# A trunk kernel on one Trainium2 core: two stage boundaries run one tile of 128 tokens at a time, in a fixed order

## The chip, the cores and the metric

The kernel runs on one core of one Trainium2 chip. The metric is the device time of one execution in microseconds (us). A core has TensorE for matrix products (PE in the profile; its weight loads are PEld), VectorE (DVE), ScalarE (ACT), GpSimd (POOL) and SyncE (SP), which here issues all the DMAs. Each engine works through its own queue in order, and waits on semaphores for the others. Results of PE land in PSUM, which has 8 banks of 128x512 f32; everything else on the chip lies in SBUF.

## The reference

Two decoder layers over 256 tokens of width 2048, batch 1, in f32. Layer 0 mixes by causal pooling, layer 1 by multi-head latent attention with 16 heads; both end in a SwiGLU FFN of width 5632. Between the layers one latent (512 wide) and one rotary key are computed from the stream and shared by all heads.

```
for i in range(DEPTH):
    shift_m, scale_m, gate_m, shift_f, scale_f, gate_f = split(silu(c) @ mod_w[i] + mod_b[i], 6)
    if i == 1:
        kv_shift, kv_scale = split(silu(c) @ kv_mod_w + kv_mod_b, 2)
        h_kv = rmsnorm(x, kv_in_norm) * (1 + kv_scale) + kv_shift
        ckv = rmsnorm(h_kv @ w_dkv, kv_norm)           # then ckv @ w_uk, ckv @ w_uv; h_kv @ w_kr is roped
    h = rmsnorm(x, norm_mix[i]) * (1 + scale_m) + shift_m
    y = pool_mixer(h) if i == 0 else mla_mixer(h, kv)  # mla_mixer ends in  o @ w_o
    x = x + gate_m * y
    h = rmsnorm(x, norm_ffn[i]) * (1 + scale_f) + shift_f
    x = x + gate_f * ((silu(h @ w_gate) * (h @ w_up)) @ w_down)
return rmsnorm(x, final_norm)
```

So at two places the whole stream x must be finished before its norm is known, and the norm before the next products can begin: from the FFN of layer 0 to the latent (`h_kv @ w_dkv`), and from attention (`o @ w_o`) to the FFN of layer 1.

## The kernel before

**Tiles.** The 256 tokens are two tiles of 128 (NT = 2), the width is four blocks of 512 (ND = 4, CH = 512). A weight block is 512x512 f32, 1 MB. It is loaded into a `raw` buffer (6 of them), and `split` makes two parts of it: `hi`, rounded by ACT to the fast format float32r (L427), and `lo`, the remainder, by DVE (L429); both go to `hl` buffers (6, three pairs). Activations are held in the same two parts. `proj_unit` (L446) multiplies one block with both token tiles: hi·hi, hi·lo, lo·hi, four products of 128x128 by 128x512 each, 12 for each tile, 24 for the block (L451). In the last block of a sum the 12 of tile 0 stand ahead of the 12 of tile 1.

**The background.** The modulation vectors need 12 products of the vector c with 2048-wide weights. They run as background units: each unit loads 1 MB into a `raw` buffer and adds it on DVE (L238, 128x2048, or L311 in two instructions of 128x1024). `split` calls `tick`, which issues units at a planned rate beside the weight blocks (`plan`, `release`, `pump`); `hold` stops it. Ahead of the latent, nine units are kept back (`MLA_LATE`) and released over the next weight blocks (`MLA_UNITS` = 6).

**The order.** Most instructions are put in order by a scheduler of the compiler, by priority and by its own model of the time; `tc.high_priority` and `urgent` raise a priority, and `tc.issue_after(ins)` puts what is traced in its block behind `ins` on the engine of `ins`. `tc.manual_schedule` keeps the written order on the engines it names. SP's queue follows the program.

**First boundary, FFN of layer 0 to latent.** `down(3)` (L656) multiplies the last two chunks of the FFN with `w_down`, for four output blocks j of two weight blocks each. After each j, `StreamEnd.piece` (L563) multiplies with the gate (L567), adds the stream (L568) and takes the sum of squares on ACT (L470), for tile 0 and then tile 1. `stat_finish` (L477) sums over the blocks for both tiles at once (L480, L474), and POOL raises to the power -0.5 (L475). `scaled` (L485) multiplies x by that (L492 on DVE when pressing, else L494 on ACT), `turned_pieces` transposes on PE (L504, 8 transposes a block), and `modulated` (L511) applies scale and shift on ACT (L518), rounds to hi (L519, ACT) and takes lo (L520, DVE), for both tiles together (128x256). The loop at L1005 runs over the four blocks of `w_dkv`, and prepares block j + 1 ahead of the products of block j. Then come the rotary key's products (L1025 to L1027) and `latent` (L1030): squares on ACT (L1034), power on POOL (L475), scaling (L1041), transposes (L504), and the two parts (L1047, L1048). `keys_values` (L1056) multiplies with `w_uk` (L1074 to L1076) and `w_uv`.

**Second boundary, attention to FFN of layer 1.** The loop at L1234 multiplies with `w_o`, four output blocks j of four weight blocks. `add_gated` (L583) is the gate, the add and the squares (L587, L588, L470). Then `stat_finish`, `scaled`, `turned_pieces`, `modulated` as above, for block 0 of the hidden stream, and `start_ffn` (L775) multiplies it with the first blocks of six chunks of `w_gate` and `w_up`. Chunk 0 keeps its four PSUM banks over all j.

Of the kernel before, what the change touches and what calls it, by code (L numbers as in the profile page):

```python
# [63 lines left out]
FFN0_UNITS, MLA_UNITS, HEAD_UNITS, WO_UNITS, FFN1_UNITS = 95, 6, 16, 8, 60  # L64
# [36 lines left out]
def tile_trunk(ctx: ExitStack, tc: tile.TileContext, a: dict, out: bass.AP):  # L101
# [278 lines left out]

    def pump(n):
        for _ in range(min(n, len(background))):
            background.pop(0).unit()
# [69 lines left out]

    def proj(src, tiles):
# [30 lines left out]
    def scaled(rstd, j, pressing=False):  # L485
        pieces = []
        for tok in range(NT):
            xr = t2k([P, CH])
            piece, scale = x[:, tok, j * CH:(j + 1) * CH], rstd[:, tok:tok + 1]
            if pressing:  # L490
                with urgent():
                    dve.tensor_scalar(out=xr, in0=piece, scalar1=scale, scalar2=None, op0=ALU.mult)  # L492
            else:
                act.activation(xr, piece, AF.Copy, scale=scale)  # L494
# [14 lines left out]
    mod_ins = [None]  # L509

    def modulated(pts, j, c_scale, c_shift):  # L511
        flush()
        t_ = act_t([P, 2, KL, T])
        with urgent() if j == 0 else nullcontext():
            for k in range(KL):
                scale, bias = (cols[:, i, j * KL + k:j * KL + k + 1] for i in (c_scale, c_shift))
                full = t2k([P, T])
                act.activation(full, pts[k // 2][:, k % 2, :], AF.Identity, scale=scale, bias=bias)  # L518
                act.activation(t_[:, 0, k, :], full, AF.Copy)  # L519
# [114 lines left out]
    def ffn(l, hT, gate_name, begun, then):  # L634
# [21 lines left out]
        def down(i):  # L656
# [6 lines left out]
            for j in range(ND):  # L663
# [4 lines left out]
                if last and j == ND - 1 and l == DEPTH - 1:  # L668
                    weights = [w_unit(wd[c * CH:(c + 1) * CH, js]) for c in g]
                    for tok in range(NT):  # L670
# [33 lines left out]
        return stat_finish() if l < DEPTH - 1 else None  # L704
# [70 lines left out]
    def start_ffn(l, first, ahead, hidden, late):  # L775

        begun = begin(l, range(BEGUN), (0,))
        hT = [first]
        with tc.issue_after(mod_ins[0].ins):
            for j in range(ND - 1):  # L780
# [4 lines left out]
                for n, (c, which) in enumerate((c, w) for c in begun for w in (GATE, UP)):  # L785
                    if n == 2 * len(begun) - 1:
                        hT.append(hidden(j + 1, pieces))
                    begun[c][which].block(j, hT[j])
# [204 lines left out]
    def then_attention():  # L993
        w_early(a["w_dkv"][0:CH, :])

    rstd = ffn(0, hT, "ffn0", begun, then_attention)


    pts = turned_pieces(scaled(rstd, 0, True))
    pieces = scaled(rstd, 1, True)  # L1000
    hkv = [modulated(pts, 0, C_AKV, C_SKV)]
    with tc.issue_after(mod_ins[0].ins):
        release(n_all, MLA_UNITS)
        ckv = [ps_t() for _ in range(NT)]
        for j in range(ND):  # L1005
            if j < ND - 1:
                pts = turned_pieces(pieces)
                if j < ND - 2:
                    pieces = scaled(rstd, j + 2)
                hkv.append(modulated(pts, j + 1, C_AKV, C_SKV))  # L1010
# [265 lines left out]
```

## Time and profile before

| | |
|---|---|
| time, median of 3 runs | 1956.19 us (1955.71 to 1956.76) |
| time of the profiled execution | 1956.75 us |
| its span, first to last instruction | 1954.6 us |
| busy: PE, DVE, ACT, POOL | 96%, 75%, 43%, 2% of the span |
| mean granted clock of PE | 0.981 |
| read from HBM | 564.98 MB, 292 GB/s over the span |

The span is 2.15 us shorter than the time of the same execution; what lies around it is outside the trace. Stages by the trace: the pooling layer to about 190 us, the FFN of layer 0 to 917 us, the latent and attention to 1202 us, the FFN of layer 1 to the end. Rows of a timeline give start, duration, engine, line, operation, output and inputs, and in brackets the idle time of the engine just before and what ended it. Rows of a table by stage give the stage, its length, then busy time and (instructions) for PE, PEld, DVE, ACT and POOL, then PE's granted clock, the share of the DMA engines and GB/s. Rows of waits give who waited for whom: us in total, times, longest. Rows of groups give busy us and mean ns of one.

### The profile page before, as it was taken

What the parts mean: (1) busy time and instruction counts of PE and PEld (TensorE: products, weight loads), DVE (VectorE), ACT (ScalarE), POOL (GpSimd) and SP (SyncE); (2) the same over time, 40 slices, a digit from 0 to 9 for tenths busy, and PEclk for the clock granted to TensorE, in tenths of its full rate; (3) what the DMA queues carried; (4) which work ended last, traced back from release to release, by engine and by line L of the source; (5) the groups of instructions that cost most, each with busy time, mean ns of one, the idle gap of its engine ahead of it and who ended that gap; (6) DMA issues with size and microseconds to landing.
All of it is one profiled execution on the core that took longest, in us unless ns stands there. A gap on an engine that the chain in (4) does not pass through costs nothing. (4 is left out here: it accounts for less than half of the span.)

```text
span 1954.6 us, 22168 instructions
## 1 busy us (share of the span) xinstructions
PE 1875.0 (96%) x8845; PEld 1519.7 (78%) x8845; DVE 1461.5 (75%) x1312; ACT 843.9 (43%) x915; POOL 30.4 (2%) x32
## 2 busy tenths in 40 slices
PE   6688999999999999998899999999999999999998
PEld 3155888888888888887789987888888888888886
DVE  1147899998788778888999975889986566654556
ACT  3023634444533334325676734544444433343333
POOL 0000000000000000000000000000000000000000
PEclk9788999999999999999999998999999999999999
DMA  9999999989898988997988684989887767665661
GB/s 396 412 415 353 387 329 331 327 302 349 320 333 291 342 306 322 344 345 243 342 312 298 231 282 150 363 295 327 292 295 257 237 219 257 237 212 187 194 219 67
DMA packets 225440, 572.71 MB, mean 293 GB/s; under 512 B 11997, under 2 KB 16421, under 8 KB 203571
## 3 DMA queue, kind: packets, MB, share of 16 engines
q1 hardware_dynamic: 225338, 571.31, 81.7%
q8 instruction: 69, 1.13, 0.2%
q14 instruction: 33, 0.27, 0.0%
HBM read 564.98 MB, written 6.29 MB: 292 GB/s over the span
## 5 line engine op out<-in xcount | busy, mean ns | idle before, releaser
L451 PE MATMUL ps<-hl,act 128*128 128x512 f32 x7008 | 1610.0, 391 | 5.7 <-ACT hl L427 2.1
L451 PEld LDWEIGHTS ps<-hl,act 128*128 128x128 f32 x7008 | 1315.6, 188 | 282.2 <-ACT act L926 3.2
L429 DVE TENSOR_TENSOR hl<-raw,hl 128x2048 fp32r<-128x2048 f32 x296 | 676.6, 2289 | 245.0 <-ACT hl L427 243.7
L427 ACT ACTIVATE hl<-raw 128x2048 fp32r<-128x2048 f32 x296 | 567.1, 1919 | 664.2 <-PE ps L451 587.7
L238 DVE SCALAR_TENSOR_TENSOR acc<-raw,s_col,acc 128x2048 f32<-128x2048 f32 x112 | 262.8, 2347 | 0.6 <-DMA raw<-in_mod_w_dram 0.4
L311 DVE SCALAR_TENSOR_TENSOR acc<-raw,s_col,acc 128x1024 f32<-128x1024 f32 x112 | 143.4, 1281 | 2.0 <-DMA raw<-in_mod_w_dram 0.7
L282 PE MATMUL ps<-raw,front 128*32 128x512 f32 x392 | 64.8, 752 | 27.6 <-DMA raw<-in_mod_w_dram 27.5
L618 DVE TENSOR_TENSOR act<-ps,act 128x512 f32<-128x512 f32 x96 | 64.1, 687 | 10.5 <-PE ps L451 10.2
L282 PEld LDWEIGHTS ps<-raw,front 128*32 128x32 f32 x392 | 9.3, 120 | 60.2 <-DMA raw<-in_mod_w_dram 48.0
L687 DVE TENSOR_TENSOR x<-ps,x 128x512 f32<-128x512 f32 x32 | 22.1, 691 | 33.3 <-PE ps L451 33.2
L470 ACT ACTIVATE junk<-x 128x512 bf16<-128x512 f32 x24 | 15.1, 630 | 59.8 <-DVE x L568 39.7
L652 ACT ACTIVATE act<-ps 128x512 fp32r<-128x512 f32 x44 | 23.6, 593 | 40.0 <-PE ps L649 36.6
L801 DVE TENSOR_TENSOR cols<-ps,front 128x16 f32<-128x16 f32 (+1 forms) x4 | 0.6, 166 | 50.9 <-PE ps L291 50.9
L696 ACT ACTIVATE t2k<-ps 128x512 f32<-128x512 f32 x24 | 14.2, 592 | 56.6 <-PE ps L451 56.6
L1074 PE MATMUL ps<-act,hl 128*128 128x256 f32 x128 | 36.9, 289 | 1.0 <-DVE hl L429 1.0
L1075 PE MATMUL ps<-act,hl 128*128 128x256 f32 x128 | 36.4, 285 | 0.0
L1076 PE MATMUL ps<-act,hl 128*128 128x256 f32 x128 | 35.9, 283 | 0.0
L700 DVE TENSOR_TENSOR t2k<-ps,t2k 128x512 f32<-128x512 f32 x24 | 16.6, 690 | 25.7 <-PE ps L451 25.5
L864 PEld LDWEIGHTS ps<-act,act 128*128 128x128 f32 x128 | 24.1, 194 | 11.4 <-issue 8.4
L864 PE MATMUL ps<-act,act 128*128 128x256 f32 x128 | 31.0, 394 | 0.0
L616 ACT ACTIVATE act<-ps 128x512 f32<-128x512 f32 x32 | 19.0, 596 | 27.2 <-PE ps L451 27.1
L518 ACT ACTIVATE t2k<-ps,cols 128x256 f32<-128x256 f32 x48 | 24.9, 575 | 12.0 <-PE ps L504 11.4
(196 smaller groups left out, 985.1 us busy)
## 6 DMA issues: line engine op xcount, KB each, us to landing
raw<-in_mod_w_dram SPq DMA_DIRECT2D x128, 1024.0 KB, 8.2
raw<-in_ffn_gate_dram SPq DMA_DIRECT2D x88, 1024.0 KB, 6.9
raw<-in_ffn_up_dram SPq DMA_DIRECT2D x88, 1024.0 KB, 5.3
raw<-in_ffn_down_dram SPq DMA_DIRECT2D x88, 1024.0 KB, 5.3
raw<-in_mod_w_dram SPq DMA_DIRECT2D x128, 512.0 KB, 6.3
raw<-in_kv_mod_w_dram SPq DMA_DIRECT2D x32, 1024.0 KB, 7.2
raw<-in_w_o_dram SPq DMA_DIRECT2D x16, 1024.0 KB, 5.7
raw<-in_w_uq_dram SPq DMA_DIRECT2D x8, 768.0 KB, 6.0
```

Of the source, the lines that this page charges most:

```text
L238: dve.scalar_tensor_tensor(out=self.acc, in0=r, scalar=s_col[:, self.kt:self.kt + 1], in1=self.acc, op0=ALU.mult, op1=ALU.add)
L282: pe.matmul(self.bank[m * STRIP:(m + 1) * STRIP, :], lhsT=weights(k), rhs=r[:, k, i, :], start=first, stop=last)
L311: dve.scalar_tensor_tensor(out=self.acc, in0=r[:, k], scalar=s_col[:, self.kt + k:self.kt + k + 1], in1=self.acc, op0=ALU.mult, op1=ALU.add)
L427: hi_ins = act.activation(hi, r, AF.Copy)
L429: lo_ins = dve.tensor_tensor(out=lo, in0=r, in1=hi.bitcast(F32), op=ALU.subtract)
L451: pe.matmul(banks[tok], lhsT=t_[:, i, k, tok * P:(tok + 1) * P], rhs=w[:, k, :], start=first and n < len(part), stop=last and n >= len(ord ...
L518: act.activation(full, pts[k // 2][:, k % 2, :], AF.Identity, scale=scale, bias=bias)
L618: dve.tensor_tensor(out=part, in0=banks[tok], in1=part, op=ALU.add)
L864: pe.matmul(mixed[g][:, n % 2, :], lhsT=wp[g][:, k, ns], rhs=pool_all[g // 2][:, g % 2, k, :], start=k == 0, stop=k == KL - 1)
L1074: pe.matmul(pt[:, h, :], lhsT=wl(h0 + h, k), rhs=t_[:, 0, k, :], start=k == 0, stop=False)
L1075: pe.matmul(pt[:, h, :], lhsT=wh(h0 + h, k), rhs=t_[:, 0, k, :], start=False, stop=False)
L1076: pe.matmul(pt[:, h, :], lhsT=wh(h0 + h, k), rhs=t_[:, 1, k, :], start=False, stop=k == KL - 1)
```

## The change

- A new function `handover` takes over both boundaries. It gets the last sums as lists (`old`: two weight blocks), finishes them for tile 0, then for tile 1, and starts the next products (`new`: two weight blocks) for tile 0 while tile 1 is still on its way. PE, ACT and DVE keep the written order inside it. The sum of squares of blocks 0 to 2 is taken ahead, so that one small DVE instruction is left for each tile, then POOL's power for that tile alone.
- In it, the transposes of one tile and block go to one PSUM bank; ACT computes hi directly from the bank (128x128, scale and shift), and a second instruction (DVE, or ACT for block 1 of tile 0) computes the full value, from which DVE takes lo in one 128x512 instruction. Block 0 is scaled on DVE, block 1 on POOL.
- At the first boundary it covers blocks 0 and 1 of `w_dkv`; at the second, block 0 of the hidden stream with chunk 0's `w_gate` and `w_up`, which `start_ffn` then leaves out.
- Blocks 2 and 3 for the latent are scaled on POOL (before: ACT) and transposed in their own turn of the loop (before: one turn ahead); block 2 uses the direct form.
- The background is held from the last block of the FFN until after `latent` (before: released ahead of the products with `w_dkv`); then it comes over `MLA_UNITS` = 4 weight blocks, and its DVE instructions stand behind latent's last one until `keys_values(1)` is issued.
- Early loads of the first blocks of `w_dkv` and of `w_gate` go; they are loaded inside `handover`.

```diff
-FFN0_UNITS, MLA_UNITS, HEAD_UNITS, WO_UNITS, FFN1_UNITS = 95, 6, 16, 8, 60
+FFN0_UNITS, MLA_UNITS, HEAD_UNITS, WO_UNITS, FFN1_UNITS = 95, 4, 16, 8, 60
...
+    behind = []
+
     def pump(n):
-        for _ in range(min(n, len(background))):
-            background.pop(0).unit()
+        with tc.issue_after(behind[-1]) if behind else nullcontext():
+            for _ in range(min(n, len(background))):
+                background.pop(0).unit()
...
+    def products(bank, t_, hi, lo, tok, first, last, swapped=False):
+
+        parts = ((hi, 0), (lo, 0), (hi, 1)) if swapped else ((hi, 0), (hi, 1), (lo, 0))
...
+    def handover(old, banks, piece, blocks, c_scale, c_shift, new):
...
+        def norm(tok):
+            v = small([P, 1])
+            dve.scalar_tensor_tensor(out=v, in0=ssq[0][:, tok, ND - 1:], scalar=1.0 / D, in1=rest[:, tok:tok + 1],
+                                     op0=ALU.mult, op1=ALU.add)
+            pool.tensor_tensor(out=rstd[:, tok:tok + 1], in0=v, in1=mhalf[:, 0:1], op=ALU.pow)
+
+        def scale(tok, j):
...
+            (dve if j == 0 else pool).tensor_scalar(out=xr, in0=src, scalar1=by, scalar2=None, op0=ALU.mult)
...
+        def hidden(tok, j):
...
+                hid_ins[0] = act.activation(hT[j][:, 0, k, tok * P:(tok + 1) * P], pt[:, k, :], AF.Identity, scale=by,
+                                            bias=plus)
...
+        def rest_of(tok, j):
...
+            mod_ins[0] = dve.tensor_tensor(out=hT[j][:, 1, :, ts_], in0=turned[tok, j][2],
+                                           in1=hT[j][:, 0, :, ts_].bitcast(F32), op=ALU.subtract)
...
+        with tc.manual_schedule(engines={mybir.EngineType.PE, mybir.EngineType.Activation, mybir.EngineType.DVE}):
+            halves.append(w_unit(new[0][3]))
+            second = raw_t([P, KL, CH])
+            sync.dma_start(second, new[1][3].rearrange("(k p) n -> p k n", p=P))
+            run(of_old(0))
...
+            piece(0)
+            norm(0)
+            halves.append((hl_t([P, KL, CH]), hl_t([P, KL, CH])))
+            act.activation(halves[1][0], second, AF.Copy)
+            scale(0, 0)
+            fs = of_old(1)
+            run(fs[:-KL])
+            turn(0, 0)
+            run(fs[-KL:])
+            hidden(0, 0)
+            if blocks > 1:
+                scale(0, 1)
+            piece(1)
+            rest_of(0, 0)
+            norm(1)
+            fs = of_new(0, 0)
+            run(fs[0])
+            if blocks > 1:
+                turn(0, 1)
+                hidden(0, 1)
+            run(fs[1] + fs[2])
+            for ks in (slice(0, 2), slice(2, KL)):
+                dve.tensor_tensor(out=halves[1][1][:, ks], in0=second[:, ks], in1=halves[1][0][:, ks].bitcast(F32),
+                                  op=ALU.subtract)
+                if ks.start == 0:
+                    scale(1, 0)
+            if blocks > 1:
+                rest_of(0, 1)
+            fs = of_new(1, 0)
+            run(fs[0] + fs[1])
+            turn(1, 0)
+            hidden(1, 0)
+            run(fs[2])
+            rest_of(1, 0)
...
+            for fs in of_new(1, 1):
+                run(fs)
+        return hT, rstd
...
-                    if last and j == ND - 1 and c == g[0]:
-                        then()
...
+        hkv, rstd = handover(old, banks, piece, 2, C_AKV, C_SKV, [(ckv, j, j == 0, dkv(j)) for j in range(2)])
...
+    pieces = scaled(rstd, 2, pool)
+    with tc.issue_after(mod_ins[0].ins), tc.issue_after(hid_ins[0].ins):
+        for j in range(2, ND):
+            pts = turned_pieces(pieces)
             if j < ND - 1:
...
+                pieces = scaled(rstd, j + 1, pool)
...
+            hkv.append(modulated(pts, j, C_AKV, C_SKV, j == 2))
...
+    release(n_all, MLA_UNITS)
+    behind.append(mod_ins[0].ins)
     kv = [keys_values(0)]
...
         if g == 1:
             plan(n_all, 0)
+            behind.clear()
...
+        hT, rstd = handover(units, banks, lambda tok: add_gated(banks[tok], gates["mla"], tok, ND - 1), 1, C_AF1, C_SF1,
+                            [(b.banks, 0, True, b.w[0:CH, :]) for b in pair])
```

In the calls, `piece(tok)` is the gate, the add and the squares of one tile, `turn(tok, j)` four transposes, and `of_new(n, tok)` three groups of four products: hi·hi, lo of the weight, lo of the activation.

More of the change, by code (lines that the diff above doesn't have):

```diff
@@ L452, in proj_unit, with product @@
                           start=first and n < len(part), stop=last and n >= len(order) - len(part))
+    def products(bank, t_, hi, lo, tok, first, last, swapped=False):
+        parts = ((hi, 0), (lo, 0), (hi, 1)) if swapped else ((hi, 0), (hi, 1), (lo, 0))
+        order = [(w, i, k) for w, i in parts for k in range(KL)]
+        def product(n, w, i, k):
+            pe.matmul(bank, lhsT=t_[:, i, k, tok * P:(tok + 1) * P], rhs=w[:, k, :], start=first and n == 0,
+                      stop=last and n == len(order) - 1)
+        return [lambda n=n, o=o: product(n, *o) for n, o in enumerate(order)]
     def proj(src, tiles):
@@ L486, in scaled @@
+    def scaled(rstd, j, engine=None):
         pieces = []
@@ L667, in down @@
                     hold()
[L668 removed]
+                if last and j == ND - 1:
                     weights = [w_unit(wd[c * CH:(c + 1) * CH, js]) for c in g]
+                    if l < DEPTH - 1:
+                        then([(mids[c], hi, lo, c == g[0]) for c, (hi, lo) in zip(g, weights)], banks,
+                             lambda tok: end.piece(banks[tok], tok, j))
+                        continue
                     for tok in range(NT):
@@ L1233, in tile_trunk @@
     stat_start()
-    for j in range(ND):
+    for j in range(ND - 1):
         if j == 0:
```

121 lines of the change are left out of this document (85 added, 36 removed).

## The prediction

> **What bounds the kernel now.** I read the page first, then the chain of waits, then the timeline at the two boundaries, then PE's waits from 880 to 1210 us.
>
> ```profile
> span 1954.6 us, 22168 instructions
> PE 1875.0 (96%) x8845; PEld 1519.7 (78%) x8845; DVE 1461.5 (75%) x1312; ACT 843.9 (43%) x915; POOL 30.4 (2%) x32
> ```
>
> PE is busy for 96%, so the time is PE's products plus what it waits. The chain that ended last runs over PE alone from the second boundary to the last output block:
>
> ```profile
> 1208.79 57.46 PE ps L451 x240
> 1271.96 0.87 PE ps L504 x8
> 1272.83 59.85 PE ps L451 x264
> ```
>
> A product at full clock takes 59.85 / 264 = 0.2267 us (24 for a block: 5.44), a transpose 0.87 / 8 = 0.109. The first row's 240 should take 54.41 and took 3.05 more: they began at half clock, as the stages there show.
>
> ```profile
> 884.00:887.00 3.00, 3.00 (x8) 2.32 (x7) 3.00 (x3) 3.00 (x3) 0.00 (x0) 0.50 0.15 57
> 957.00:963.00 6.00, 4.56 (x21) 3.87 (x22) 6.00 (x7) 3.50 (x6) 0.00 (x0) 0.72 0.95 358
> 1204.70:1214.90 10.20, 8.08 (x23) 6.28 (x24) 6.26 (x8) 6.17 (x11) 0.69 (x1) 0.51 0.06 9
> ```
>
> PE's last product, the transposes, and the first product behind them, at the first boundary and then at the second:
>
> ```profile
> 914.78 2.66 PE L451 MATMUL ps<-hl,act 128*128 128x512 f32 x11
> 921.45 3.46 PE L504 MATMUL ps<-con,t2k 128*128 128x128 f32 x16 [4.01 <-DVE t2k L492]
> 924.67 5.89 PE L451 MATMUL ps<-hl,act 128*128 128x512 f32 x24
> ```
> ```profile
> 1199.83 2.20 PE L451 MATMUL ps<-hl,act 128*128 128x512 f32 x9
> 1206.04 1.97 PE L504 MATMUL ps<-con,t2k 128*128 128x128 f32 x8 [4.02 <-DVE t2k L492]
> ```
>
> First boundary: 7.23 us from 917.44 to 924.67, of which 16 transposes need 1.74, so 5.49 lost; 0.45 more in the first 24 products (5.89 for 5.44). Second: 1202.03 to 1208.79 is 6.76, less 0.87, so 5.89, and the 3.05 of half clock: 8.94. Between them PE waits, with the background at work, where the latent is normalised:
>
> ```profile
> PE ps L504 <- DVE t2k L1041: 3.2, 2, 3.1
> PE ps L1074 <- DVE hl L429: 1.0, 1, 1.0
> PE ps L1025 <- DVE hl L1018: 0.5, 1, 0.5
> ```
>
> The 0.5 belongs to the loop over `w_dkv`: 6.4 us for the first boundary. The latent loses 3.2 + 1.0, and the half clock: 0.28 of 6 us in its stage, 1.7 at most, less what PE idled in it; I take 1.5. That makes 5.7.
>
> **The handover, step by step.** What follows the last product at the first boundary, before:
>
> ```profile
> 917.48 0.69 DVE L567 TENSOR_TENSOR x<-ps,gate 128x512 f32<-128x512 f32 x1 [1.08 <-PE ps L451]
> 918.20 0.69 DVE L568 TENSOR_TENSOR x<-x,act 128x512 f32<-128x512 f32 x1
> 918.99 0.63 ACT L470 ACTIVATE junk<-x 128x512 bf16<-128x512 f32 x1 [1.77 <-DVE x L568]
> 919.52 0.19 ACT L470 ACTIVATION_READ_ACCUMULATOR junk<-x 128x1 f32 x1
> 919.74 0.16 DVE L480 TENSOR_REDUCE sm<-ssq 128x2 f32<-128x8 f32 x1 [0.85 <-ACT junk L470]
> 919.94 0.17 DVE L474 TENSOR_SCALAR sm<-sm 128x2 f32<-128x2 f32 x1
> 920.19 0.69 POOL L475 TENSOR_TENSOR rstd<-sm,mhalf 128x2 f32<-128x2 f32 x1 [61.59 <-DVE sm L474]
> 920.91 1.67 DVE L492 TENSOR_SCALAR t2k<-x,rstd 128x512 f32<-128x512 f32 x4 [0.81 <-POOL rstd L475]
> ```
>
> Set the end of tile 0's old products to 0. The same steps, with one small DVE instruction in place of two (0.2 less), have the scaled tile ready at 3.8. PE has tile 1's first 20 products meanwhile, 4.53, so the transposes start without a wait; were that cover gone, the price is the 4.01 above. Then the four transposes (0.44) and the last four old products (0.91) end at 5.88, while ACT makes the first hi. The other prices:
>
> ```profile
> L518 ACT ACTIVATE t2k<-ps,cols 128x256 f32<-128x256 f32 x48 | 24.9, 575 | 12.0 <-PE ps L504 11.4 <-DVE cols L342 0.6
> L1161 DVE SCALAR_TENSOR_TENSOR t2k<-ps,con 128x128 f32<-128x128 f32 x32 | 8.5, 285 | 0.3 <-ACT t2k L1159 0.3
> L1018 DVE TENSOR_TENSOR hl<-raw,hl 128x1024 fp32r<-128x1024 f32 x2 | 2.4, 1224 | 0.0
> ```
>
> DVE makes four full values of 128x128 (about 0.3 each) by 6.1, tile 1's gate and add (1.4) by 7.5, tile 0's lo (0.7) by 8.2. PE needs that lo at 8.1 (first boundary, one more set of four transposes ahead of it) or 7.7 (second): waits of 0.1 and 0.5. Tile 1's squares end at 8.2 and its small DVE step at 8.5; then DVE's written order goes on with half of the second weight's lo (1.22), and POOL's power stands beside it. Its price there is in the latent's rows:
>
> ```profile
> 952.80 0.17 DVE L474 TENSOR_SCALAR sm<-sm 128x2 f32<-128x2 f32 x1
> 952.92 2.35 DVE L238 SCALAR_TENSOR_TENSOR acc<-raw,s_col,acc 128x2048 f32<-128x2048 f32 x1
> 953.04 2.78 POOL L475 TENSOR_TENSOR sm<-sm,mhalf 128x2 f32<-128x2 f32 x1 [32.17 <-DVE sm L474]
> 955.19 2.28 DVE L429 TENSOR_TENSOR hl<-raw,hl 128x2048 fp32r<-128x2048 f32 x1
> 957.39 1.40 DVE L1041 TENSOR_SCALAR t2k<-ps,sm 128x512 f32<-128x512 f32 x2
> ```
>
> The power took 0.69 with DVE idle, 2.78 beside L238, which reads two tensors of SBUF, and ended just behind it. So I let it end 0.6 behind the half, at 10.3; tile 1's scaling (1.67 / 4 = 0.42) and, queued behind it on DVE, the other half (1.22) follow, to 12.1 with the 0.03 to 0.1 that the rows show between steps. PE has 8.2, four products of tile 0 with the first weight's second part (0.91), four with the second weight (0.91) and two with the first half (0.45): it is at 10.5 and waits 1.6. With a power of 0.69 the wait is 0.8, with 2.78 it is 2.5. Sum for a handover: 1.7 at the first boundary, 2.1 at the second (bounds 0.9 to 3). Later tile-1 steps lie under 12 to 24 products still queued.
>
> **The loop over blocks 2 and 3.** Transposes now stand in their own turn, so PE waits for the first hi: one L518 (0.6) for block 2, two ACT steps (up to 1.15) for block 3: 1.7, below it if the scheduler pulls the transposes ahead; I take 1.2 (0 to 3). Scaling goes to POOL, for which no row exists: a write-only memset of 128x512 bounds it below, and a full wait behind DVE (2.78) above:
>
> ```profile
> L1091 POOL MEMSET krT<- 128x512 f32 x1 | 0.5, 528 | 19.2 <-DVE t2k L916 19.2
> ```
>
> Block 1's scaling has 3 us until its transposes, block 2's and 3's have over 5, so at 0.8 each, nearer the memset as DVE's one-source L492 takes 0.42, they cost nothing; at 2.78 each, 1 us, inside the bounds above. First boundary: 6.4 - 1.7 - 1.2 = 3.5 won (1 to 6). Second: 8.94 - 2.1 = 6.8 (4 to 8); behind it the chain is PE alone, so it counts in full. Of its moved loads, `w_gate`'s now follows four `w_o` loads; 21.8 us of products of that output block hide it, and if not, it costs its landing:
>
> ```profile
> raw<-in_ffn_gate_dram SPq DMA_DIRECT2D x88, 1024.0 KB, 6.9
> ```
>
> **The background.** The last squares of the latent, and the first transposes:
>
> ```profile
> 950.51 0.60 ACT L1034 ACTIVATE junk<-ps 128x512 bf16<-128x512 f32 x1 [1.86 <-PE ps L451]
> 958.28 0.41 PE L504 MATMUL ps<-con,t2k 128*128 128x128 f32 x2 [3.08 <-DVE t2k L1041]
> ```
>
> The rotary key's products kept PE until 958.28 - 3.08 = 955.2, so they cover some 4 us behind the squares. Without L238 beside it the chain there is 0.17, then 0.69 to 2.78, then 1.40: 2.3 to 4.4, just under that cover. What stays is the wait for the first hi and lo behind the transposes, about 1.3: 5.7 - 1.3 = 4.4 won (2 to 5.5). But the units come later:
>
> ```profile
> L238 DVE SCALAR_TENSOR_TENSOR acc<-raw,s_col,acc 128x2048 f32<-128x2048 f32 x7 | 16.4, 2348 | 0.0
> 961.00:1120.00 159.00, 156.09 (x1000) 141.23 (x1000) 149.07 (x222) 110.70 (x231) 4.62 (x3) 1.00 0.83 285
> ```
>
> Seven ran from 922 to 961; these 16.4 us of DVE now fall into a stage where DVE had 159 - 149.1 = 9.9 us free. On SP their loads now stand between those of `w_uk` and `w_uv`, which wait for a `raw` buffer until DVE has worked off the units ahead. Upper end: 16.4 - 9.9 = 6.5 on PE's path. Lower end 0: PE was busy for 156.1 of 159 with DVE at 94%, so a lag was hidden. I take 2.5, nearer that end. Seven loads more at 285 / 0.83 = 343 GB/s are 21 us in 27 us of free DMA time.
>
> **The clock.** After 880 us PE waits once for 1.90 us and is then at half clock for at least the 3.0 us of the first stage row; after the 1.0 at L1074 it isn't (stage at 1.00).
>
> ```profile
> 882.81 1.43 PE L451 MATMUL ps<-hl,act 128*128 128x512 f32 x4 [1.90 <-ACT hl L427]
> ```
>
> My waits of 1.6 are nearer 1.90. Half of 3.0 us and a little more, 1.7, is lost each time; I count one of the two handovers.
>
> [...]
>
> **The sum**, against the profiled execution: 3.5 + 6.8 + 4.4 - 2.5 - 1.7 = 10.5 won; 1956.75 - 10.5 = 1946.25. The median of the runs lies 0.56 below that execution: 1945.7.
>
> **The rivals.** (1) Neither handover loses the clock, as with the 1.0 wait: 1.7 less, 1944.0. For it: the gaps are shorter than 1.90. (2) DVE is the bound behind the latent: 6.5 in place of 2.5, 1949.7. For it: 94% busy there. (3) The wait only changes its name: ACT's copy of the second weight stands ahead of tile 0's hi, and a load 4 us late stops all engines. Then the first boundary wins nothing, the second its 3.05 of clock, the latent 4.4, less 6.5: 1.0 won, 1955.2. Against it: the second `w_dkv` block's load went out 21 us ahead of the boundary.
>
> ```profile
> 896.16 0.37 SPq L440 DMA_DIRECT2D raw<-in_w_dkv_dram  x1
> ```
>
> (4) Slower: all nine held units stand on PE's path, each load of a key or value weight behind two of them in the `raw` buffers. 9 x 2.348 = 21.1 against 3.5 + 6.8 + 4.4 - 1.7 = 13.0: 8.1 lost, 1964.3. It decides from 13.0 / 2.348 = 5.5 units on. Against it: the 9.9 us free, and six buffers' lead. (5) The order written isn't the order that runs, and the boundaries stay as they were: about 1956.2.
>
> **How the numbers follow.** Chances: forecast 0.45, (1) 0.28, (2) 0.10, (3) 0.10, (4) 0.04, (5) 0.03. A measurement of this kernel can tell about 0.2%, 3.9 us. Faster are the forecast, (1) and (2), 0.83; same (3) and (5), 0.13; slower (4), 0.04. The range leaves out (3) to (5), 0.17, and ends between (2) and (3), at 1953; below, with no clock loss, nothing given back, and each handover 1.2 better, it is 1945.7 - 1.7 - 2.5 - 2.4 = 1939.1, so 1938.5.
>
> **What would show it.** Right: PE's idle before L504's successors falls from 4.0 to none at each boundary; no stage at half clock for 10 us near 1200; POOL's power in the latent with no L238 beside it; seven L238 more behind the latent; PE waits of 0.8 to 2.5 on the second weight's lo. Wrong: PE waiting for ACT's copy of that weight inside the handover, or for `w_uk` and `w_uv` behind the latent by over 7 us.

## The result, and the profile after

The changed kernel takes 1967.89 us (median of 6 runs, 1966.03 to 1969.11), the kernel before 1956.41 us (6 runs, 1955.71 to 1957.26). The ratio is 1.0059, with a 95% interval of 1.0049 to 1.0070: 11.5 us slower, where 10.5 less was forecast. The profiled execution took 1967.68 us. Its page begins:

```profile
span 1965.9 us, 22192 instructions
PE 1875.9 (95%) x8845; PEld 1517.4 (77%) x8845; DVE 1471.6 (75%) x1334; ACT 840.1 (43%) x911; POOL 42.2 (2%) x40
```

PE's busy time is the same to 0.9 us, so nearly all of the loss is waiting. Marks in both traces show where it comes in:

| start of | before | after | after is |
|---|---|---|---|
| the last products of layer 0's FFN | 906.56 | 905.92 | 0.6 ahead |
| the latent's squares | 948.0 | 947.5 | 0.5 ahead |
| the first products with `w_uk` | 960.3 | 957.4 | 2.9 ahead |
| the last copy of the first group's values | 974.9 | 969.1 | 5.8 ahead |
| the squares of the query latent (products with `w_dq`) | 1020.1 | 1033.3 | 13.2 late |
| the last products with `w_o` | 1191.15 | 1204.14 | 13.0 late |
| the FFN's first row of 264 products | 1272.83 | 1283.68 | 10.9 late |

The first handover wins nothing. The latent wins 2.4 up to the first products with `w_uk`, and 5.3 up to the copies behind the first group of `w_uk` and `w_uv`, which include, in the kernel before, the wait of 1.0 at L1074 and the end of the half clock (granted 0.57 from 958.28 to 962.28, 1.00 from 963 on):

```profile
974.88 0.60 ACT L1066 ACTIVATE act<-ps 128x512 f32<-128x512 f32 x1 [0.99 <-PE ps L451]
```
```profile
969.10 0.60 ACT L1199 ACTIVATE act<-ps 128x512 f32<-128x512 f32 x1 [0.53 <-PE ps L455]
```

The second handover wins some 2. In between, from 969 to 1033, 19 us go, where the change issues only the units that it held. PE's longest waits from 900 to 1245, in the changed kernel:

```profile
PE ps L328 <- DVE acc L324: 11.1, 1, 11.1
PE ps L464 <- DVE act L546: 4.3, 4, 1.9
PE ps L1207 <- DVE hl L433: 3.1, 1, 3.1
PE ps L1207 <- ACT act L1180: 1.8, 1, 1.8
PE ps L464 <- DVE hl L584: 1.0, 1, 1.0
```

The first row is a wait that the kernel before doesn't have. DVE behind the latent, and what PE does meanwhile:

```profile
962.78 0.48 DVE L1181 SCALAR_TENSOR_TENSOR act<-ps,vcol,act 128x256 fp32r<-128x256 f32 x1
963.17 14.28 DVE L238 SCALAR_TENSOR_TENSOR acc<-raw,s_col,acc 128x2048 f32<-128x2048 f32 x6
977.38 2.28 DVE L433 TENSOR_TENSOR hl<-raw,hl 128x2048 fp32r<-128x2048 f32 x1
979.58 9.51 DVE L238 SCALAR_TENSOR_TENSOR acc<-raw,s_col,acc 128x2048 f32<-128x2048 f32 x4
989.12 2.31 DVE L322 STREAM_TRANSPOSE raw<-acc 128x2048 f32<-128x2048 f32 x1
991.47 2.29 DVE L324 TENSOR_REDUCE acc<-raw 128x64 f32<-128x2048 f32 x1
994.53 0.72 DVE L342 SCALAR_TENSOR_TENSOR cols<-ps,vcol 32x16 f32<-32x16 f32 x4 [0.78 <-PE ps L328]
995.28 2.29 DVE L433 TENSOR_TENSOR hl<-raw,hl 128x2048 fp32r<-128x2048 f32 x1
```
```profile
981.67 1.03 PE L627 MATMUL ps<-con,t2k 128*128 128x128 f32 x8
993.81 0.69 PE L328 MATMUL ps<-acc,con 128*128 128x64 f32 x2 [11.10 <-DVE acc L324]
997.63 0.58 PE L1207 MATMUL ps<-act,hl 128*128 128x256 f32 x1 [3.13 <-DVE hl L433]
```

The held units are ten, and they are the last ten of the sum that gives a scale vector (C_AM1). That vector is needed for block 0 of attention's hidden stream, behind the second group of `w_uk` and `w_uv`: PE is there at 982.7. The sum's fold (L322, L324) ends at 993.8. The small product that finishes it (L328) stands in PE's queue in front of everything else, so PE waits 11.1 us; the next weight's lo, behind the units on DVE, costs 3.1 more, and PE then runs at a granted clock of 0.50 to 1002.0: 21 products of 128x256 take 4.62 us from 997.63, some 2.1 more than at the 0.118 from one product's start to the next behind 1002.25. The sum is in the rows of DVE: ten units (23.8), one weight's lo (2.3) and the fold (4.6) fill it from 963.2 to 993.8, and PE needed the last of it at 982.7. Two stretches show what happened to DVE. Before, from its first unit to the end of the fold, and after, from the first handover's last lo to the latent's and on to the end of the fold (PE, PEld, DVE, ACT, POOL; clock; DMA; GB/s):

```profile
929.25:976.41 47.16, 42.20 (x241) 36.30 (x240) 47.05 (x37) 28.66 (x46) 2.78 (x1) 0.96 0.97 349
```
```profile
933.72:963.17 29.45, 27.23 (x162) 23.29 (x161) 21.91 (x27) 19.81 (x31) 1.14 (x2) 1.00 0.49 179
963.17:993.76 30.59, 18.56 (x119) 16.22 (x117) 30.23 (x14) 8.50 (x10) 0.00 (x0) 0.86 0.95 358
```

Before, DVE was busy for 47.05 of 47.16 us up to the end of the fold, the units spread between the instructions of the main work, and the fold was ready at 976.4. After, it stands idle for 7.5 of 29.45 us ahead of the latent, with the DMA engines at half load, and the ten units come behind one another, in front of all that PE needs next.

The second handover does part of what was forecast. The rows of PE there, then of DVE:

```profile
1214.11 0.60 PE L529 MATMUL ps<-con,t2k 128*128 128x128 f32 x4
1214.47 3.27 PE L464 MATMUL ps<-hl,act 128*128 128x512 f32 x12
1219.63 4.71 PE L464 MATMUL ps<-hl,act 128*128 128x512 f32 x12 [1.90 <-DVE act L546]
```
```profile
1216.29 1.36 DVE L540 TENSOR_SCALAR t2k<-ps,cols 128x128 f32<-128x128 f32 x4 [2.94 <-ACT act L536]
1217.57 0.68 DVE L714 TENSOR_TENSOR t2k<-ps,gate 128x512 f32<-128x512 f32 x1
1218.29 0.69 DVE L715 TENSOR_TENSOR x<-x,t2k 128x512 f32<-128x512 f32 x1
1218.89 0.69 DVE L546 TENSOR_TENSOR act<-t2k,act 128x512 fp32r<-128x512 f32 x1
```

The transposes start without a wait, and the 4.0 us are gone. But DVE stands idle for 2.94 us until ACT has read the bank four times (1.50 us from 1214.75), only then makes the full values, the other tile's gate and add, and the lo that PE waits for. The wait is 1.90, and the twelve products behind it take 4.71 in place of 2.72 (granted clock 0.63 over the 4 us from 1219.63).

### The profile page after: what moved, and what is told of

Read it like the earlier page. It is cut to its first block, busy times and chain, and to the rows that moved or that the text cites. A ratio compares the mean times of both kernels' runs of the same rounds, so it can differ in the third digit from the quotient of the medians.

```text
span 1965.9 us, 22192 instructions
## 1 busy us (share of the span) xinstructions
PE 1875.9 (95%) x8845; PEld 1517.4 (77%) x8845; DVE 1471.6 (75%) x1334; ACT 840.1 (43%) x911; POOL 42.2 (2%) x40
## 4 chain that ended last, share of the span: by engine, by line
PE 83%; DVE 5%; issue 5%; DMA 5%; ACT 2%; POOL 0%; SPq 0%; POOLq 0%; DVEq 0%; ACTq 0%
PE ps L455 72%; DMA raw<-in_mod_w_dram 4%; PE ps L282 1%; PE ps L993 1%; DVE acc L238 1%; DVE acc L311 1%; PE ps L464 1%; PE ps L776 1%; DMA raw<-in_ffn_gate_dram 1%; DVE hl L433 1%; PE ps L1207 1%; PE ps L1209 1%; PE ps L1208 1%; PE ps L1321 0%; ACT hl L431 0%
## 5 line engine op out<-in xcount | busy, mean ns | idle before, releaser
L238 DVE SCALAR_TENSOR_TENSOR acc<-raw,s_col,acc 128x2048 f32<-128x2048 f32 x112 | 262.8, 2347 | 1.2 <-DMA raw<-in_mod_w_dram 0.8
```

Of the source, the lines that this page charges most:

```text
L238: dve.scalar_tensor_tensor(out=self.acc, in0=r, scalar=s_col[:, self.kt:self.kt + 1], in1=self.acc, op0=ALU.mult, op1=ALU.add)
```

## The experiments

Ratios are against the kernel before, on the same chip, with 95% intervals.

**First question: the units' date, their place, or the fixed order?** `a1_early` releases them ahead of the loop over `w_dkv`, as before, though over 4 weight blocks in place of 6; `a2_hold` puts the hold and the late release alone into the kernel before; `a3_notdue` holds units of the next vector, which has no date nearby; `a4_later` moves the consumer behind the third group of `w_uk` and `w_uv`.

```diff
# a1_early (a2_hold: the opposite, in the kernel before)
+        release(n_all, MLA_UNITS)
         for j in range(2, ND):
...
-    release(n_all, MLA_UNITS)
-    behind.append(mod_ins[0].ins)
# a3_notdue
-    plan(n_all + MLA_LATE, FFN0_UNITS)
+    plan(n_all, FFN0_UNITS)
-    release(n_all, MLA_UNITS)
+    release(n_all - MLA_LATE, MLA_UNITS)
# a4_later
+        if g > 1:
...
-        hmx.append(modulated(pts, g - 1, C_AM1, C_SM1))
+            hmx.append(modulated(pts, g - 2, C_AM1, C_SM1))
```

> The changed kernel, but the background is released where it was before, ahead of the loop over the w_dkv blocks (over 4 weight blocks), and its DVE instructions stand behind nothing. Everything else of the change stays. Theory T (the held units carry a due time: the scale vector that they end in is needed for block 0 of attention's hidden stream, its fold stands in PE's queue and comes late; about 11.1 us of wait, 3.1 behind it and 2.4 of half clock, 16.6 in all): the wait of PE's L328 for the fold goes, POOL's power in the latent has L238 beside it again (2 to 3 us given back): 1949 to 1955. Rival R (the handovers' own fixed order costs the time): 1963 or more. Rival D (the units cost DVE the same wherever they run in this stretch): 1960 to 1966.

> The kernel before, with nothing of the change but the background: held from the last FFN block until after the latent, then over 4 weight blocks, its DVE instructions behind the latent's last one. T: the 16.6 us come, less some 3 us that the latent wins: 1966 to 1973. R: within 2 us of the kernel before, 1954.5 to 1958.5. D: 1960 to 1966.

> The changed kernel, but the due part is finished in the FFN (nine units more there), and the nine units that run behind the latent are of the next part, attention's gate, which nothing needs until the products with w_o. Same number of units, same place, same order of release; only the due time is gone. T: PE's wait for the fold goes, 1949 to 1956 (the FFN may lose a little by nine more units). D (the weight on DVE is what costs, due or not): 1963 to 1968, with PE waiting for the lo parts of w_uk and w_uv. R: 1963 or more.

> The changed kernel, but block 0 of attention's hidden stream (the consumer of the scale vector), with the fold's product on PE in front of it, is traced one group of w_uk and w_uv later; the units stay held as in the change. T: the 11.1 us of wait at the fold go or shrink to under 2, since some 48 products of 128x256 and those of a w_uv block stand ahead of it: 1951 to 1957. D: PE waits about as long for the lo part of the next w_uk block instead, 1963 to 1968. R: 1963 or more.

Measured: `a1_early` 1967.95 (1.0064, 1.0050 to 1.0077), `a2_hold` 1968.07 (1.0067, 1.0054 to 1.0080), `a3_notdue` 1982.84 (1.0139, 1.0125 to 1.0153), `a4_later` 1967.52 (1.0064, 1.0051 to 1.0076). The theory of the date alone (T) falls: `a1_early` and `a3_notdue` have no wait for a late fold, and lose as much or more. The fixed order of the handovers (R) falls with `a2_hold`, which came as T said: the hold makes the whole loss without any handover. Of the other two, `a4_later` lies in D's range, while `a1_early` and `a3_notdue` lie above those of T and D. In `a4_later` the wait only changes its name, as D said:

```profile
PE ps L1207 <- DVE hl L433: 14.2, 1, 14.2
```

With the fold's product out of the way, PE waits as long for the lo of the next weight, which stands behind the same units on DVE (it ends at 996.2, the units and the fold having kept DVE from 963.4). In `a3_notdue` the latent's squares start at 955.9, 8.4 us later than in the changed kernel: nine units more cost that much in the FFN. Behind the latent the loss grows by another 5.3 (the query latent's squares start at 1047.0, 13.7 later), though only the first of the units there has a date. And `a1_early` gets rid of the wait for the fold, but gets others, in the loop and the latent:

```profile
PE ps L455 <- ACT act L642: 4.0, 2, 2.3
PE ps L1208 <- DVE hl L433: 3.2, 1, 3.2
PE ps L627 <- DVE t2k L1175: 2.4, 2, 2.2
PE ps L455 <- DVE act L647: 2.2, 1, 2.2
```

**Second question: DVE's adds or the loads?** `b4_narrow` keeps loads and buffers and adds 64 columns; `d3_noload` keeps the adds, of a part of the stream, and drops the loads; `d1_skip` drops both; `d2_before_skip` drops both in the kernel before.

```diff
# b4_narrow (narrow[0] is set for the held units)
-            dve.scalar_tensor_tensor(out=self.acc, in0=r, ...
+            n = slice(0, 64 if narrow[0] else D)
+            dve.scalar_tensor_tensor(out=self.acc[:, n], in0=r[:, n], ...
# d3_noload (skip[0] likewise)
-            r = raw_t([P, D])
-            sync.dma_start(r, self.w[self.kt * P:(self.kt + 1) * P, :])
+            if skip[0]:
+                r = x[:, 0, :]
+            else:
+                r = raw_t([P, D])
...
```

> The changed kernel, but the units held until behind the latent add only 64 of the 2048 columns of each load (this leaves out part of one scale vector's sum); their loads, buffers and order stay. Some 23 us of DVE's work go there. D: PE's waits of 11.1 and 3.1 us and the half clock behind the latent go, 1947 to 1953. Rival S (the loads, in SP's queue and in the raw buffers ahead of w_uk and w_uv, hold PE up): 1962 or more.

> The changed kernel, whose ten held units add all 2048 columns, but from a part of the stream that lies in SBUF, so that their loads and their raw buffers are gone and DVE's work stays (one scale vector has other values). With the run that kept the loads and cut the adds at 1960.0: L, both count: 1957 to 1963, PE's wait for the fold shrinks to 3 to 7 us. If DVE's work alone makes the loss: 1965 or more. If the blocked buffers alone make it: 1948 to 1952.

> The changed kernel without the ten units that it holds until behind the latent (their loads and their adds are left out, so one scale vector lacks ten sixteenths of its sum; fold and consumer stay). Theory L (the held units cost twice: their loads sit in the raw buffers and stop SP's queue from 943 to 963 us, and their adds come on top of a full DVE): all of PE's waits behind the latent go, and what is left is the handovers' win of about 3 us at the first boundary and the latent and 2.4 at the second: 1946 to 1951. Rival R (the handovers cost the time themselves): 1956 or more.

> The kernel before without the same ten units (loads and adds left out, in the same way), as the mate of the changed kernel without them. L: in the kernel before these units ran in DVE's gaps around the boundary and cost next to nothing but the latent's wait beside L238: 1952 to 1956; the changed kernel without them is 4 to 7 us below this one. R: the changed kernel without them is no faster than this one.

Measured: `b4_narrow` 1960.00 (1.0023, 1.0014 to 1.0032), `d3_noload` 1966.94 (1.0053, 1.0040 to 1.0065), `d1_skip` 1955.17 (0.9995, 0.9986 to 1.0004), `d2_before_skip` 1957.32 (1.0003, 0.9994 to 1.0012). `d3_noload` lies in the range of DVE's work alone, and `d1_skip` and `d2_before_skip` 4.2 and 1.3 above theory L's. So the ten units cost 1967.89 - 1955.17 = 12.7 us in the changed kernel, and nothing that can be measured in the time of the kernel before. (In the trace of `d2_before_skip` the query latent's squares start at 1017.4, 2.8 ahead of the kernel before, but the second boundary's transposes at 1207.3, 1.3 late: what is won is given back behind, for a reason that these runs don't show.) The adds alone make nearly all of it, 1966.94 - 1955.17 = 11.8: without the loads PE still waits 9.0 us in front of the fold's product, under another line number. The view names no releaser; the fold on DVE ends at 993.3, and the product starts at 993.4:

```profile
PE ps L333 <- issue: 9.0, 1, 9.0
```

Without the adds 4.8 us of it stay (1960.00 - 1955.17), between the two ranges that were expected, and there the units wait for their loads, which go out from 962 on, once the `raw` buffers come free:

```profile
978.03 0.28 DVE L241 SCALAR_TENSOR_TENSOR acc<-raw,s_col,acc 128x64 f32<-128x64 f32 x1 [1.70 <-DMA raw<-in_mod_w_dram]
980.56 0.28 DVE L241 SCALAR_TENSOR_TENSOR acc<-raw,s_col,acc 128x64 f32<-128x64 f32 x1 [2.25 <-DMA raw<-in_mod_w_dram]
```

The two costs lie side by side, as 11.8 and 4.8 are more than 12.7 together, and DVE's is the longer. The pair without units also shows what the rest of the change is worth: 1957.32 - 1955.17 = 2.1 us, less than the 4 to 7 expected, and rough, as the two intervals overlap.

**Third question: what does each boundary win?** `b1_second` and `c1_first` change one boundary in the kernel before; in `c1_first` the units are released behind the handover, over 6 weight blocks. `e3_delay` has that delay alone. `b2_actfull` is the changed kernel with full values on ACT.

```diff
# e3_delay, in the kernel before
-        release(n_all, MLA_UNITS)
...
+            if j == 2:
+                release(n_all, MLA_UNITS)
             hi, lo = w_unit(a["w_dkv"][j * CH:(j + 1) * CH, :])
# b2_actfull (the other branch is ACT's)
-                if j == 0 or tok == 1:
+                if False:
                     dve.tensor_scalar(out=full[:, k, :], ...
# b2_actfull and f2_c1_indirect
-            hkv.append(modulated(pts, j, C_AKV, C_SKV, j == 2))
+            hkv.append(modulated(pts, j, C_AKV, C_SKV))
```

> The kernel before, with the second boundary alone changed (attention to the last FFN); the first boundary and the background stay as before. Theory D (formed after the first four runs: from the FFN's last block to the query latent the sum of DVE's work sets the time; it was busy for 100.8 of 113.5 us before and 108.1 of 127.4 after, because held units leave DVE idle at the boundary and then come on top of a full engine): nothing of that is in this kernel, and the second handover loses 5.4 instead of 8.9: 1951 to 1954. Rival M (what the second handover wins is given back by 1267 us, where the loads run at 374 GB/s and the DMA engines are full): 1955 to 1957.

> The kernel before, with the first boundary's handover and the new loop over w_dkv, and the background released right behind the handover over 6 weight blocks as before; the second boundary stays as before. D: DVE has some 7 us more to do (the full values that ACT made before) and no unit runs beside the handover, so 1962 to 1969. Rival H (only the later release costs, the handover itself wins): 1952 to 1956.

> The changed kernel, but all full values are made on ACT, as before the change (L540 goes to ACT, block 2 takes the indirect form): 6.2 us less for DVE between the first boundary and the query latent. D: a good part of that comes back although ACT's chain in the handover is longer by some 0.6 for each tile: 1961 to 1965. Rival R (the latency of the handover's steps counts): 1968 to 1972.

> The kernel before, with nothing changed but that the background is released at the third w_dkv block, over 6 weight blocks, as in the run that changed the first boundary alone (1963.2). If the delay alone makes that run's loss: 1961 to 1966. If the first handover itself makes it: 1955.5 to 1958.

Measured: `b1_second` 1953.48 (0.9989, 0.9980 to 0.9998), `c1_first` 1963.24 (1.0034, 1.0022 to 1.0047), `b2_actfull` 1966.08 (1.0053, 1.0039 to 1.0067), `e3_delay` 1958.09 (1.0010, 1.0001 to 1.0018). The second boundary wins 2.4 us alone. The first costs 7.3, of which the delay is 1.7. That lies in D's range, but not for D's reason: `b2_actfull` moves little, outside both of its ranges, so the weight of the full values on DVE isn't the main thing. In the rows of `c1_first` another stands out, in block 2 of the loop, where ACT makes hi and DVE the full value from the same bank:

```profile
934.69 1.02 ACT L645 ACTIVATE act<-ps,cols 128x256 fp32r<-128x256 f32 x2 [2.27 <-PE ps L630]
937.82 0.56 ACT L645 ACTIVATE act<-ps,cols 128x256 fp32r<-128x256 f32 x1 [2.10 <-DVE t2k L646]
941.32 0.56 ACT L645 ACTIVATE act<-ps,cols 128x256 fp32r<-128x256 f32 x1 [2.94 <-DVE t2k L646]
```
```profile
937.25 0.53 DVE L646 TENSOR_SCALAR t2k<-ps,cols 128x256 f32<-128x256 f32 x1
937.70 2.34 DVE L238 SCALAR_TENSOR_TENSOR acc<-raw,s_col,acc 128x2048 f32<-128x2048 f32 x1
940.30 0.99 DVE L646 TENSOR_SCALAR t2k<-ps,cols 128x256 f32<-128x256 f32 x2
```

ACT's next read waits for DVE's (2.10 and 2.94 us), and DVE's stands behind a unit of 2.34 us. `f2_c1_indirect` takes only this form away.

> The kernel with the first boundary alone changed (1963.2), but block 2 of w_dkv takes the indirect form (ACT alone reads the bank: full value, then hi). If the direct form is what costs (ACT waits for DVE's read of the shared bank, and that read stands behind a background unit of 2.34 us; PE then waited 1.7, 2.3 and 2.1 us): those three waits fall to under 2 in all, 1957.5 to 1960. If DVE's work or the handover itself costs: within 1.5 of 1963.2.

Measured: 1959.52 (1.0017, 1.0008 to 1.0026). The form costs 3.7 us with units about; what remains of the first boundary is 1.4 above the delay alone, which these runs don't tell from nothing. The rate of release counts too: up to the query latent `a1_early` and `c1_first` differ in little else (4 weight blocks against 6), and its squares start at 1030.5 and 1026.1. No run changes the rate alone.

**Fourth question: which step of the handover is too long?** All but `e2_skip_order` start from `b1_second`. `d4_restfirst` writes tile 0's lo ahead of tile 1's piece. `e1_order` writes tile 1's piece ahead of tile 0's full values, and moves further steps on DVE and PE. `e2_skip_order` has that in both handovers of `d1_skip`. `e5_b1_twobanks` gives each tile's transposes two banks; `e4_twobanks` is `e1_order` with them.

```diff
# e1_order (hi_of and full_of are the two halves of hidden)
-            hidden(0, 0)
-            piece(1)
-            rest_of(0, 0)
-            norm(1)
+            hi_of(0, 0)
+            piece(1)
+            full_of(0, 0)
+            norm(1)
+            rest_of(0, 0)
+            if blocks == 1:
+                scale(1, 0)
...
-            run(fs[1] + fs[2])
+            run(one[1] + two[0] + one[2])
# e5_b1_twobanks
-                pe.transpose(pt[:, k, :], xr[:, k * P:(k + 1) * P], ident)
+                pe.transpose(pt[k // 2][:, k % 2, :], xr[:, k * P:(k + 1) * P], ident)
```

> The kernel before with the second boundary alone changed, and in its handover tile 0's lo (rest_of) written ahead of tile 1's gate, add and squares on DVE. PE's wait of 1.9 us for that lo shrinks to about 0.5 and the half clock behind it (some 1.7 us) goes, while tile 1's chain comes 0.7 later: 1950 to 1952.5. Rival (tile 1's chain is the next to bind, so the wait only moves): within 0.7 of 1953.5.

> The kernel before with the second boundary alone changed, and its handover in another order: on DVE tile 1's gate and add ahead of tile 0's full values (DVE stood idle for 2.9 us there, behind ACT), tile 1's scaling ahead of the second weight's lo; on PE the second weight's first products ahead of those that need tile 0's lo. Theory O (the order of DVE's steps was the mis-sized part): waits at this boundary fall from 1.9 + 0.7 and a half clock of some 1.7 to about 1.4 in all: 1949.5 to 1952. Rival P (something else, the loads or the weight's split, is next to bind): within 1 of 1953.5.

> The changed kernel without the ten held units, with the same other order in both handovers (at the first boundary only DVE's: tile 1's gate and add ahead of tile 0's full values). O: 2 to 4 us less than the 1955.2 without the new order: 1951 to 1953.5. P: 1954 to 1956.5.

> The kernel before with the second boundary alone changed, in the changed kernel's order, but each tile's four transposes go to two PSUM banks, two to each, so that DVE can read the first while ACT reads the second. If the shared bank put DVE's full values behind all four of ACT's: DVE starts some 0.7 us earlier and PE's waits for tile 0's and tile 1's lo fall from 1.9 and 0.7 to about 1.2 and 0.2, the half clock perhaps with them: 1950.5 to 1953. If DVE's order or ACT's chain holds it back in another way: the waits stay, within 1 of 1953.5.

> The version that beat both kernels at 1950.8 (second boundary alone, tile 1's piece ahead of tile 0's full values, and so on), with the four transposes in two PSUM banks as well. If the bank still stands in the chain: 0.5 to 1.5 less, 1949.3 to 1950.3. If the new order already fills the time behind ACT (PE's waits there were 0.5 and 0.2): within 0.5 of 1950.8.

Measured: `d4_restfirst` 1955.92 (0.9996, 0.9987 to 1.0006), `e1_order` 1950.78 (0.9972, 0.9961 to 0.9983), `e2_skip_order` 1951.17 (0.9977, 0.9967 to 0.9987), `e5_b1_twobanks` 1951.64 (0.9975, 0.9965 to 0.9985), `e4_twobanks` 1949.45 (0.9967, 0.9954 to 0.9979). The last four came as their theories said. In `d4_restfirst` the wait only moves to the second weight's lo (2.7 us in two waits); its time lies above both expected ranges, though the ratio's interval overlaps that of `b1_second`, and its trace, taken of the fastest execution (1953.49), doesn't show why. In `e5_b1_twobanks` DVE begins 0.84 us behind ACT's first read, where in the changed kernel it was 1.54 (ACT's row there begins at 1214.75, DVE's at 1216.29):

```profile
1199.68 1.50 ACT L532 ACTIVATE act<-ps,cols 128x128 fp32r<-128x128 f32 x4 [0.71 <-PE ps L525]
1200.52 1.43 DVE L536 TENSOR_SCALAR t2k<-ps,cols 128x128 f32<-128x128 f32 x4 [2.02 <-ACT act L532]
1203.93 2.56 PE L460 MATMUL ps<-hl,act 128*128 128x512 f32 x10 [1.26 <-DVE act L542]
```

In `e1_order` DVE does the other tile's piece in that time, and PE's waits at the boundary shrink to 0.5 and 0.2, with no half clock (26 products in 6.19 us):

```profile
1202.85 0.69 DVE L731 TENSOR_TENSOR t2k<-ps,gate 128x512 f32<-128x512 f32 x1 [2.32 <-PE ps L460]
1204.18 1.36 DVE L540 TENSOR_SCALAR t2k<-ps,cols 128x128 f32<-128x128 f32 x4
1206.32 1.20 PE L460 MATMUL ps<-hl,act 128*128 128x512 f32 x4 [0.51 <-DVE act L546]
1209.52 6.19 PE L460 MATMUL ps<-hl,act 128*128 128x512 f32 x26 [0.17 <-DVE hl L593]
```

So two cures are shown, two banks (all runs of `e5_b1_twobanks` lie below all of `b1_second`) and the new order. `e1_order` moves steps of DVE and of PE together, so what DVE's order is worth by itself stays open, and in the trace of `b1_second` a half clock of some 1.7 us stands behind the wait of 1.90, as it doesn't behind the same wait in `d1_skip` (more on it below). `e4_twobanks` is the fastest version run, 6.6 us below the kernel before; its interval overlaps that of `e1_order`, so that the two cures add up is not shown. Without units, the first handover in the new order adds nothing that can be measured to the second (1951.17 against 1950.78).

## Why the prediction was wrong

**The background: the step that failed.** The prediction took 2.5 of bounds 0 to 6.5, since DVE had 9.9 us free from 961 to 1120. The units cost 12.7. It counted free time over 159 us, but all ten units (23.8 us) stood in DVE's queue in front of the fold, and in front of the lo that PE needed behind it. DVE had 19.5 us from its first unit to the moment when PE needed the fold, and 30.6 us of work for them; the rest is PE's wait of 11.1. What the units sum up to, and for which step, stood in the code. The date isn't all of it: with a later date PE waits as long for the lo (`a4_later`), and units with no date cost no less (`a3_notdue`). The prediction also took the time that the units left at the boundary for time won, when before they filled DVE's gaps there (47.05 of 47.16 us busy) at no cost in the time (1957.32 without them in `d2_before_skip`). The count was right: ten ran behind the latent, three of which did so before, so seven more. The loads, which it put at 21 us in 27 free, cost 4.8 without the adds. Its own sign of being wrong, PE waiting for `w_uk` and `w_uv` behind the latent by over 7 us, came in another form: 11.1 for the fold, then 3.1 for the lo.

**Rival (4)**, slower with the held units on PE's path at 1964.3, is nearest to what happened, in sign and mechanism. Both reasons against it failed: the 9.9 us were in the wrong place, and the six buffers gave no lead, as held units kept five of them: in `b4_narrow` five narrow adds run at once at 962.1, and the sixth waits 3.1 us for its load.

**The first boundary** was to win 3.5, and won nothing: 0.6 ahead at its start, 0.5 at the latent. Its first handover lost 5.4 us of PE's time (905.92 to 934.85, less 23.5 of products and transposes) in place of 1.7. The transposes were to start without a wait and waited 0.77, as tile 0's gate stood behind a weight's lo on DVE (to 913.3). The wait for tile 0's lo, put at 0.1, was 1.46: DVE's four full values were put beside ACT's first hi, ending at 6.1; they came behind all four of ACT's (these ran from 917.80 to 919.30, DVE's from 919.34). The wait for the second weight's lo, put at 1.6, was 1.04. One of 0.26 came on tile 1, and the remaining 1.9 lie in steps of 0.1 to 0.4 between the short groups of products and transposes, for which the sum has no term. POOL's scaling was put at 0.8, nearer the memset; it took

```profile
916.63 1.86 POOL L524 TENSOR_SCALAR t2k<-x,rstd 128x512 f32<-128x512 f32 x1
924.70 2.91 POOL L524 TENSOR_SCALAR t2k<-x,rstd 128x512 f32<-128x512 f32 x1
```

the 1.86 with DVE idle from 917.05 on, and the 2.91, above the upper bound of 2.78, where DVE's lo of the second weight (L584, 1.22 from 925.04) ran beside it, but no transpose waited for it. The loop over blocks 2 and 3 lost about the 1.2 forecast, as long as no unit ran there.

**The second boundary** was to win 6.8 less 1.7 of clock and won 2.4 alone; the term that was too small is the same, ACT's reads of the bank (1.50) and DVE's behind them (1.36) one after the other, with the piece queued behind both: a wait of 1.9 + 0.7 and the half clock. Behind it the chain wasn't PE alone, as PE waits 0.82 more for a weight's lo at 1267.7. That the half clock came at one of the two handovers (at the first the granted clock was 1.00 over the 4 us behind the wait of 1.46) agrees with the sum, but the wait of 1.90 isn't enough by itself, as the prediction read from one row: at the same place twelve products took 4.62 us behind 1.91 in `b4_narrow` and 4.64 behind 1.90 in `d3_noload`, while in `d1_skip` ten took 2.56, at full clock:

```profile
1206.58 2.56 PE L471 MATMUL ps<-hl,act 128*128 128x512 f32 x10 [1.90 <-DVE act L553]
```

With the order changed the boundary gives 5.6 (1956.34 - 1950.78), near the forecast, but that is another order than the one forecast.

**The latent** was to win 4.4 (2 to 5.5); it won 5.3 up to the copies at 969.1, and the units took it back. POOL's power has no L238 beside it, as forecast, and took 0.72 at 952.49; the latent's hi and lo cost 1.8, forecast 1.3.

The step list had DVE's full values beside ACT's first hi. In the rows DVE's idle time (2.29 us at the first handover, 2.94 at the second) ends with ACT's four reads of the same bank, and with two banks in `e5_b1_twobanks` DVE began 0.84 behind ACT's first read in place of 1.54, 0.7 earlier. A list with the full values behind the hi would have had that time.

## What to carry to other kernels

Before moving work that fills gaps, find what will stand behind it in its engine's queue, the step that reads its result and the other steps that PE needs, and count the engine's work up to there, not its free time over the whole stage. A boundary that is idle on one engine may be where another engine catches up (here DVE, busy for 47.05 of the 47.16 us from 929.25); run the kernel without the background on both sides, and the price of the move and the gain of the new order come apart. And where a second engine's read of a bank begins only behind the first one's, as DVE's here 1.54 us behind the start of ACT's, write the second engine's next independent step into that time: `e1_order`, which does this and moves other steps too, has PE waits of 0.5 and 0.2 there in place of 1.9 and 0.7.

## What the runs showed of the hardware

- PE's clock: in the kernel before, a wait of 1.90 us for a weight's hi (to 882.81) was followed by a granted clock of 0.60 over the next 4 us; in the changed kernel the same wait of 1.90 (to 882.97) was followed by 1.00. At the second handover a wait of 1.90 was followed by 0.63 in the changed kernel (12 products in 4.71 us), and one of the same length by full clock in `d1_skip` (10 in 2.56). Behind a wait of 2.06 in `c1_first` 34 products took 7.99 us, and behind one of 2.50 in `b2_actfull` 16 took 3.92: 0.235 and 0.245 each, near the 0.227 of full clock. So in these traces the length of the wait alone doesn't decide.
- POOL's power of one column took 0.55 us with DVE idle beside it (at 915.98 and 1212.28 in the changed kernel), and 1.48 and 1.47 (at 923.12 and 1220.06) beside DVE's L584, which reads two tensors, `raw` and `hl`, and took 1.22.
